# A block's seven products on TensorE reordered, so that two which share a PSUM bank never follow each other; one low part ahead of the last output sum

## The chip, the cores and the metric

The kernel runs on one core of one Trainium2 chip. The metric is the device time of one execution in microseconds; the median of three runs of the kernel before is 1206.51 us (1204.94 to 1207.25).

## The reference, cut to what matters

Two layers of a latent-token backbone, 512 tokens of width 1024. Each layer is a mixer with a gated residual and then a SwiGLU channel mixer (inner width 2816, which is 22 tiles of 128). The change is in the SwiGLU of the second layer:

```
def swiglu(h, w1, w3, w2):
    return (jax.nn.silu(h @ w1) * (h @ w3)) @ w2
...
        x = x + g2 * swiglu(modulate(rms_norm(x, norm2_g[i]), sh2, sc2), ffn_w1[i], ffn_w3[i], ffn_w2[i])
```

## The kernel before, in words

All matrices are fp32. A product is made from three TensorE matmuls per 128 rows of contraction: each operand is split into a high part (a rounded copy, made by ScalarE: "hi") and a low part (source minus high part, made by VectorE: "lo"), and hi·hi, hi·lo and lo·hi are summed in PSUM.

The function `ffn_blocks` does the second layer's SwiGLU. Of the 22 tiles of the inner width the first 3 are computed directly; for the other 19 (called blocks) `w1` and `w3` are taken together. A block is a 2 by 2 scheme of Strassen's kind: the two row blocks are `w3` and `w1`, the contraction of 1024 is cut in halves, and the 512 tokens are cut in halves (left and right, 256 each). It needs seven products instead of eight, each of 4 × 3 = 12 matmuls of 128×256. One call of `block_window` emits one block's window. `prod` emits the 12 matmuls of one product (line 1193 in every case, so a trace tells products apart by their tiles).

A window takes three PSUM tiles of one bank each (128×512 fp32): `b1` holds c11 in its left half; `b2` holds m6 in its left half and m7 in its right half; `b3` holds m5. In the order before the products are

1. c11 = a11 · left half of h (bank b1), copied out by ScalarE (line 1213)
2. m6 = s2 · T2 (bank b2), taken off q by VectorE (line 1217)
3. m5 = s1 · T1 (bank b3)
4. m7 = s3 · T3 (bank b2, right half), added into c by VectorE (line 1222); m5 is added into c as well (line 1223)
5. m6 = a22 · T4 (bank b2, left half again, a new sum), added into c by VectorE (line 1226)
6. c11 += a12 · left half of h (bank b1), through Silu on ScalarE (line 1229)
7. m5 += s4 · right half of h (bank b3); its reader (line 1234) is emitted in the next window

The text calls the fifth product "m6 again", the sixth "c11 again" and the seventh "m5 again". They are the second uses of their PSUM halves.

In the same window the weights of the next block are prepared by the list `prep` (seven steps, by index): 0 the high part of a11 and a12 (line 1133); 1 and 2 the sum s24 on VectorE (lines 1137 and 1140); 3 the low part of a11 and a12 (line 1144); 4 hi and lo of s2 and s4 (lines 96 and 97, whi and wlo of 128×1024); 5 hi and lo of s1 and s3 (lines 96 and 97); 6 hi and lo of a22 (lines 96 and 97, tile u, 128×512, in the buffers named wraw). Step 0 of the block after next is called as `after()`. `tail` holds the last three steps of the block before (lines 1234 to 1244: second Silu, product with c, hi and lo of the result).

The blocks stand in three segments of 5, 7 and 7 windows (SEGS). After each segment follow eight products with `w2` (`down`, lines 116 to 118, 24 matmuls of 128×512 or 21). In the last window of a segment, which has no next block in the segment, `prep` loads and splits the first two `w2` units instead (lines 1176 and 1180), and its step 6 is empty.

The work of this stretch is not reordered by the scheduler: `tc.manual_schedule()` is entered ahead of it, and each engine runs its instructions in the order in which the code emits them. The framework puts the semaphore waits; it tracks PSUM by tile, that is by bank, not by the half that is read.

Of the kernel before, what the change touches and what calls it, by code (L numbers as in the profile page):

```python
# [12 lines left out]
AF = mybir.ActivationFunctionType  # L13
# [8 lines left out]
HS = 256  # L22
# [39 lines left out]
def tile_dit(  # L62
# [5 lines left out]
    V, A, G, T = nc.vector, nc.scalar, nc.gpsimd, nc.tensor  # L68
# [14 lines left out]
    def ps(shape=(P, S)):  # L83
        return pp.tile([P, S], F32, tag="ps", name=nm("ps"))

    def t2k(n=S):
        return tmp.tile([P, n], F32, tag="t", bufs=TB, name=nm("t"))
# [4 lines left out]
    def f32(ap):  # L92
        return ap.bitcast(F32)
# [202 lines left out]
    for k in range(KT):  # L296
        q = acc0 if k == 0 else t2k()
# [748 lines left out]
    def ffn_blocks(l, nrm, head, sq_next=None, make_next=None):  # L1046
# [4 lines left out]
        left, right = (0, HS), (HS, S)  # L1051
# [10 lines left out]
        def gslot(f):  # L1062
            i = next(f - a for a, n in SEGS if a <= f < a + n)
            if GSL[l][i // 2] == 6:
                gt[f] = slot(("6a", "6b")[i % 2], [P, 2, S], F32R)
            elif i % 2 == 0:
                d = slot(GSL[l][i // 2], [P, 2, 2, S], F32R)
                gt[f], gt[f + 1] = d[:, 0], d[:, 1]
            return gt[f]
# [52 lines left out]
        def prep_block(f):  # L1122

            w = wf[f] = {}
            raw, s13 = raws[f], sums[f]
            a22, a11, a12 = (raw[:, q, :] for q in range(3))

            def pair(u, x, y):
                w[x], w[y] = view(u, 0), view(u, S)

            def a():
                w["ua"] = ua = hilo()
                A.copy(ua[0], raw[:, 1:3, :].rearrange("p q c -> p (q c)"))

            def b():
                w["s24"] = units.tile([P, D], F32, tag="wraw", bufs=RB, name=nm("s24"))
                V.tensor_add(w["s24"][:, :S], s13[:, :S], a11)

            def c():
                V.tensor_add(w["s24"][:, S:], a12, w["s24"][:, :S])  # L1140

            def d():
                ua = w.pop("ua")
                V.tensor_sub(ua[1], raw[:, 1:3, :].rearrange("p q c -> p (q c)"), f32(ua[0]))
                pair(ua, "a11", "a12")

            def e():
                u = hilo()
                split(*u, w.pop("s24"))
                pair(u, "s2", "s4")  # L1150

            def g():
                u = hilo()
                split(*u, s13)
                pair(u, "s1", "s3")

            def h():
                u = units.tile([P, 2, S], F32R, tag="wraw", bufs=RB, name=nm("u22"))
                split(u[:, 0, :], u[:, 1, :], a22)
                w["a22"] = view((u[:, 0, :], u[:, 1, :]), 0)  # L1160

            return [a, b, c, d, e, g, h]
# [25 lines left out]
        def prod(o, wv, bv, start=True):  # L1188
            for kk in range(4):
                wh, wl = wv(kk)  # L1190
                bh, bl = bv(kk)
                for i, (w, b) in enumerate(((wh, bh), (wh, bl), (wl, bh))):
                    T.matmul(o, w, b, start=start and kk == 0 and i == 0, stop=kk == 3 and i == 2, skip_group_check=True)  # L1193
# [4 lines left out]
        def block_window(f, tail, prep, after):  # L1198

            w = wf.pop(f)  # L1200
            hh, hl = nrm.h

            def h_op(x, half):
                return lambda kk: (hh(4 * x + kk, *half), hl(4 * x + kk, *half))

            b1, b2, b3 = ps(), ps(), ps()
            c11, m6, m7, m5 = b1[:, :HS], b2[:, :HS], b2[:, HS:], b3[:, :HS]
            q, c = t2k(), t2k()
            tail[0]()
            prep[1]()  # L1210
            tail[1]()
            prod(c11, w["a11"], h_op(0, left))
            A.copy(q[:, HS:], c11)
            prep[2]()
            tail[2]()
            prod(m6, w["s2"], st["T2"])
            V.tensor_sub(q[:, :HS], q[:, HS:], m6)
            prep[3]()
            prep[4]()
            prod(m5, w["s1"], st["T1"])  # L1220
            prod(m7, w["s3"], st["T3"])
            V.tensor_add(c[:, HS:], q[:, :HS], m7)  # L1222
            V.tensor_add(c[:, :HS], c[:, HS:], m5)
            prep[5]()
            prod(m6, w["a22"], st["T4"])
            V.tensor_add(c[:, HS:], c[:, HS:], m6)
            prep[6]()
            prod(c11, w["a12"], h_op(1, left), False)
            A.activation(q[:, HS:], c11, AF.Silu)
            after()  # L1230
            prod(m5, w["s4"], h_op(1, right), False)

            def t0():
                V.tensor_add(q[:, :HS], q[:, :HS], m5)
                A.activation(q[:, :HS], q[:, :HS], AF.Silu)

            def t1():
                V.tensor_mul(c, c, q)

            def t2():  # L1240
                d = gslot(f)
                for o, i in ((HS, 0), (0, HS)):
                    A.activation(d[:, 0, o:o + HS], c[:, i:i + HS], AF.Identity, scale=-1.0)
                    V.scalar_tensor_tensor(d[:, 1, o:o + HS], c[:, i:i + HS], -1.0, f32(d[:, 0, o:o + HS]), ALU.mult, ALU.subtract)

            return [t0, t1, t2]
# [19 lines left out]
        for a, n in SEGS:  # L1266
# [8 lines left out]
            for f in range(first, a + n):  # L1275
                i = blk.index(f)
                load_sums(i + 3)
                load_raw(i + 2)
                if f == a + n - 1:
                    prep = wprep  # L1280
                else:
                    prep = nxt_prep or prep_block(f + 1)
                    if nxt_prep is None:
                        prep[0]()
                nxt_prep = None
                after = nothing
                if f + 2 < a + n:
                    nxt_prep = prep_block(f + 2)
                    after = nxt_prep[0]
                elif f + 2 == a + n:  # L1290
                    wload, wprep = two_units(wu, [w2src(0), w2src(1)], n * P)
                    after = wload
                tail = block_window(f, tail, prep, after)
# [262 lines left out]
```

## Time and profile before

| | before |
|---|---|
| median of 3 runs | 1206.51 us |
| the profiled execution's own time | 1206.65 us |
| its span (first to last instruction) | 1204.7 us |
| TensorE busy | 1177.0 us (98%) |
| VectorE busy | 802.3 us (67%) |
| ScalarE busy | 478.3 us (40%) |
| second uses of m6 that waited for line 1222 | 19 of 19 |

Busy time of TensorE is the sum over matmuls whose rows overlap (a matmul of 128×256 has a row of 0.28 us, and the next one starts 0.12 us after it), so it says little on how densely they stand. What can be read with more trust is the time from the start of one matmul to the start of another.

### The profile page before, as it was taken

What the parts mean: (1) busy time and instruction counts of PE and PEld (TensorE: products, weight loads), DVE (VectorE), ACT (ScalarE), POOL (GpSimd) and SP (SyncE); (2) the same over time, 40 slices, a digit from 0 to 9 for tenths busy, and PEclk for the clock granted to TensorE, in tenths of its full rate; (3) what the DMA queues carried; (4) which work ended last, traced back from release to release, by engine and by line L of the source; (5) the groups of instructions that cost most, each with busy time, mean ns of one, the idle gap of its engine ahead of it and who ended that gap; (6) DMA issues with size and microseconds to landing.
All of it is one profiled execution on the core that took longest, in us unless ns stands there. A gap on an engine that the chain in (4) does not pass through costs nothing.

```text
span 1204.7 us, 16804 instructions
## 1 busy us (share of the span) xinstructions
PE 1177.0 (98%) x6627; PEld 992.8 (82%) x6627; DVE 802.3 (67%) x1302; ACT 478.3 (40%) x787; POOL 128.0 (11%) x110
## 2 busy tenths in 40 slices
PE   8999999999999999999999999999999999999998
PEld 6787856569988888888888888889998899889987
DVE  7989877657665556554443799967876467647752
ACT  5545455435332323332222554335644234324430
POOL 1013300000000000000004485100000000000000
PEclk9999999999999999999999999999999999999999
DMA  9872033383365565555455232221377156725332
GB/s 350 300 293 78 1 117 98 111 269 124 90 213 188 192 209 190 182 181 166 166 166 156 72 105 90 84 88 53 108 181 211 44 151 160 203 72 141 88 104 90
DMA packets 52226, 177.24 MB, mean 147 GB/s; under 512 B 5682, under 2 KB 6578, under 8 KB 51891
## 3 DMA queue, kind: packets, MB, share of 16 engines
q1 hardware_dynamic: 49410, 166.21, 41.7%
q0 software_dynamic: 2736, 9.96, 4.9%
q8 instruction: 52, 0.85, 0.3%
q14 instruction: 28, 0.22, 0.1%
HBM read 174.05 MB, written 2.10 MB: 146 GB/s over the span
## 4 chain that ended last, share of the span: by engine, by line
PE 92%; DVE 4%; DMA 2%; ACT 1%; issue 1%; POOL 0%; SPq 0%; DVEq 0%; ACTq 0%
PE ps L116 21%; PE ps L118 21%; PE ps L117 21%; PE ps L1193 16%; PE ps L866 2%; PE ps L708 1%; PE ps L581 1%; PE ps L851 1%; PE ps L852 1%; PE ps L853 1%; PE ps L871 1%; DMA s<-in_w 1%; DVE t L211 1%; PE ps L822 1%; PE ps L197 1%; DVE t L1222 1%
## 5 line engine op out<-in xcount | busy, mean ns | idle before, releaser
L116 PE MATMUL ps<-s,whi 128*128 128x512 f32 (+1 forms) x1067 | 394.6, 370 | 1.2 <-DVE x L272 1.2
L117 PE MATMUL ps<-s,whi 128*128 128x512 f32 (+1 forms) x1067 | 390.9, 366 | 2.1 <-DVE s L217 2.1
L118 PE MATMUL ps<-s,wlo 128*128 128x512 f32 (+1 forms) x1067 | 390.6, 366 | 0.4 <-DVE wlo L97 0.4
L96 ACT CAST whi<-wraw 128x1024 fp32r<-128x1024 f32 (+2 forms) x127 | 129.5, 1024 | 281.8 <-PE ps L117 138.1
L116 PEld LDWEIGHTS ps<-s,whi 128*128 128x128 f32 x1067 | 201.6, 189 | 35.7 <-DVE x L272 1.6
L117 PEld LDWEIGHTS ps<-s,whi 128*128 128x128 f32 x1067 | 201.7, 189 | 35.4 <-DVE s L217 2.3
L118 PEld LDWEIGHTS ps<-s,wlo 128*128 128x128 f32 x1067 | 201.6, 189 | 34.6 <-DVE wlo L97 0.9
L97 DVE TENSOR_TENSOR wlo<-wraw,whi 128x1024 fp32r<-128x1024 f32 (+2 forms) x107 | 127.1, 1188 | 80.1 <-ACT whi L96 76.6
L1193 PE MATMUL ps<-s,whi 128*128 128x256 f32 x912 | 165.2, 283 | 0.0
L1193 PEld LDWEIGHTS ps<-s,whi 128*128 128x128 f32 x912 | 142.4, 192 | 0.3
L1193 PE MATMUL ps<-s,wlo 128*128 128x256 f32 x456 | 129.0, 283 | 0.0
L272 DVE SCALAR_TENSOR_TENSOR x<-ps,m_g,x 128x512 f32<-128x512 f32 (+1 forms) x67 | 43.9, 661 | 105.7 <-PE ps L118 105.7
L154 DVE CUSTOM_DVE_ANT_0 ada<-ada,scb,vec 128x1024 f32<-128x1024 f32 x80 | 100.1, 1279 | 1.4 <-DMA ada<-in_ada 1.4
L1193 PEld LDWEIGHTS ps<-s,wlo 128*128 128x128 f32 x456 | 87.5, 192 | 0.0
L1120 POOL DMA_DIRECT2D s<-in_w x19 | 16.8, 885 | 598.6 <-DMA s<-in_w 436.5
L1008 DVE TENSOR_TENSOR t<-ps,t 128x512 f32<-128x512 f32 x22 | 15.2, 692 | 71.3 <-PE ps L118 71.3
L96 ACT CAST whi<-s 128x1024 fp32r<-128x1024 f32 x38 | 39.6, 1044 | 54.0 <-PE ps L1193 28.1
L1369 DVE SCALAR_TENSOR_TENSOR ps<-s,vec,ps 128x512 f32<-128x512 f32 x78 | 55.8, 749 | 1.4 <-ACT ps L1366 0.9
L97 POOL TENSOR_TENSOR wlo<-wraw,whi 128x1024 fp32r<-128x1024 f32 x20 | 49.0, 2454 | 31.2 <-ACT whi L96 27.2
L117 PE MATMUL ps<-s,s 128*128 128x256 f32 (+1 forms) x160 | 50.2, 315 | 0.0
L118 PE MATMUL ps<-s,s 128*128 128x256 f32 (+1 forms) x160 | 50.1, 314 | 0.0
L116 PE MATMUL ps<-s,s 128*128 128x256 f32 (+1 forms) x160 | 48.3, 317 | 0.2 <-ACT s L216 0.2
(278 smaller groups left out, 1661.0 us busy)
## 6 DMA issues: line engine op xcount, KB each, us to landing
ada<-in_ada SPq DMA_DIRECT2D x82, 512.0 KB, 4.4
wraw<-in_w SPq DMA_DIRECT2D x74, 512.0 KB, 3.6
s<-in_w SPq DMA_DIRECT2D x19, 768.0 KB, 5.7
wraw<-in_w_in SPq DMA_DIRECT2D x20, 512.0 KB, 3.3
s<-in_w SPq DMA_DIRECT2D x38, 256.0 KB, 4.0
s<-in_w POOLq DMA_DIRECT2D x19, 512.0 KB, 5.4
s<-in_ada SPq DMA_DIRECT2D x16, 512.0 KB, 6.7
wraw<-in_w_out SPq DMA_DIRECT2D x16, 512.0 KB, 3.8
```

The source lines that it names most:

```text
L96: A.copy(hi, src)
L97: (eng or V).tensor_sub(lo, src, f32(hi))
L116: T.matmul(o, wh, ah, start=start, stop=False)
L117: T.matmul(o, wh, al, start=False, stop=False)
L118: T.matmul(o, wl, ah, start=False, stop=stop)
L154: i = V.tensor_tensor_reduce(raw, raw, scv, 1.0, vc("ada_b", idx), ALU.mult, ALU.add, accum_out=dst)
L272: V.scalar_tensor_tensor(X[m][:, a:b], psum, gcol, X[m][:, a:b], ALU.mult, ALU.add)
L866: T.matmul(p[64 * x:64 * x + 64, :], vh[t][:, 2 * j + x, :], ost["p", 2 * j + x, tp][:, s * S:(s + 1) * S], start=(t == 0), stop=(t == 5))
L1008: V.tensor_mul(g, p, held.pop(f))
L1120: G.dma_start(s13, w[:, :D], accum_op=ALU.add)
L1193: T.matmul(o, w, b, start=start and kk == 0 and i == 0, stop=kk == 3 and i == 2, skip_group_check=True)
L1369: V.scalar_tensor_tensor(dst, cp[:, w:w + S], vec[:, o + w:o + w + 1], src, ALU.mult, ALU.add)
```

## The change

It moves the sixth product, c11 again, with its Silu, ahead of the fifth, m6 again. `prep[6]()` (hi and lo of a22 for the next block) now stands ahead of m6 again instead of behind it, so on VectorE the low part of a22 comes ahead of the sum that reads m6.

```diff
             V.tensor_add(c[:, HS:], q[:, :HS], m7)
             V.tensor_add(c[:, :HS], c[:, HS:], m5)
             prep[5]()
+            prod(c11, w["a12"], h_op(1, left), False)
+            A.activation(q[:, HS:], c11, AF.Silu)
+            prep[6]()
             prod(m6, w["a22"], st["T4"])
             V.tensor_add(c[:, HS:], c[:, HS:], m6)
-            prep[6]()
-            prod(c11, w["a12"], h_op(1, left), False)
-            A.activation(q[:, HS:], c11, AF.Silu)
             after()
             prod(m5, w["s4"], h_op(1, right), False)
```

Since lines move, the Silu of c11 is line 1226 in the changed kernel and line 1229 before, and the sum that reads m6 is line 1229 in the changed kernel and line 1226 before.

On TensorE, in the third window of the first segment (ps_7546 is bank b1 with c11, ps_7547 is b2 with m6 and m7, ps_7548 is b3 with m5; the tile u is a22), this stood before between the last matmul of m7 and the first of m5 again:

```order
L1193 MATMUL ps_7547<-s_1187_7213,wlo_7493 128x256
L1193 MATMUL ps_7547<-s_1188_7214,u_1237_7509 128x256 [waits DVE_49,Activation_49]
L1193 MATMUL ps_7547<-s_1190_7216,u_1237_7509 128x256
...
L1193 MATMUL ps_7546<-s_1135_6765,whi_7398 128x256 [waits Activation_49]
L1193 MATMUL ps_7546<-s_1137_6767,whi_7398 128x256
...
L1193 MATMUL ps_7548<-s_1135_6765,whi_7462 128x256 [waits DVE_49]
```

And this stands there now, at the same place of the same window:

```order
L1193 MATMUL ps_7547<-s_1187_7213,wlo_7493 128x256
L1193 MATMUL ps_7546<-s_1135_6765,whi_7398 128x256 [waits Activation_49]
L1193 MATMUL ps_7546<-s_1137_6767,whi_7398 128x256
...
L1193 MATMUL ps_7547<-s_1188_7214,u_1237_7509 128x256 [waits DVE_49]
L1193 MATMUL ps_7547<-s_1190_7216,u_1237_7509 128x256
...
L1193 MATMUL ps_7548<-s_1135_6765,whi_7462 128x256 [waits DVE_49]
```

The twelve matmuls into b1 now stand between the last matmul of m7 and the first of m6 again, which is the one that waits for VectorE; no matmul is added or removed.

On VectorE, behind the sum of m5 in the same window (t_7550 is c, u_1253 the next block's a22), the difference is:

```order
 L1223 TENSOR_TENSOR t_7550<-t_7550,ps_7548 128x256
 L97 TENSOR_TENSOR wlo_7620<-s_1207_7291,whi_7619 128x1024
-L1226 TENSOR_TENSOR t_7550<-t_7550,ps_7547 128x256
 L97 TENSOR_TENSOR u_1253_7636<-s_1225_7417,u_1253_7636 128x512
+L1229 TENSOR_TENSOR t_7550<-t_7550,ps_7547 128x256
 L1234 TENSOR_TENSOR t_7549<-t_7549,ps_7548 128x256
 L1137 TENSOR_TENSOR s_1263_7680<-s_1224_7413,s_1241_7544 128x512
```

The sum that reads m6 moved behind the low part of a22. On ScalarE, at the same place of the window (ps_7546 is c11, t_7549 is q), the difference is:

```order
 L96 CAST whi_7589<-s_1247_7553 128x1024
 L96 CAST whi_7619<-s_1207_7291 128x1024
+L1226 ACTIVATE t_7549<-ps_7546 128x256
 L96 CAST u_1253_7636<-s_1225_7417 128x512
-L1229 ACTIVATE t_7549<-ps_7546 128x256
 L1133 CAST whi_7652<-s_1241_7544 128x1024
 L1235 ACTIVATE t_7549<-t_7549 128x256
```

The Silu of c11 moved ahead of the high part of a22.

## Rows read from the trace of the kernel before

**Rows 1.** Page: shares of the chain that ended last, by engine.

```profile
PE 92%; DVE 4%; DMA 2%; ACT 1%; issue 1%; POOL 0%; SPq 0%; DVEq 0%; ACTq 0%
```

**Rows 2.** Waits of TensorE: waiter, releaser, us in total, times, longest us.

```profile
PE ps L1193 <- DVE t L1222: 11.8, 19, 0.9
```

**Rows 3.** Chain that ended last, first segment: start us, us, what.

```profile
898.33 0.43 DVE t L1222
898.89 10.31 PE ps L1193 x84
```

**Rows 4.** Timeline of TensorE, one window: start us, us, instruction, count, [idle before].

```profile
898.01 0.28 PE L1193 MATMUL ps<-s,wlo 128*128 128x256 f32 x1
898.89 1.66 PE L1193 MATMUL ps<-s,u 128*128 128x256 f32 x12 [0.60 <-DVE t L1222]
900.39 0.40 PE L1193 MATMUL ps<-s,whi 128*128 128x256 f32 x2
...
908.91 0.28 PE L1193 MATMUL ps<-s,wlo 128*128 128x256 f32 x1
```

**Rows 5.** Timeline of the weight loads at the same place.

```profile
897.89 0.19 PEld L1193 LDWEIGHTS ps<-s,wlo 128*128 128x128 f32 x1
898.86 0.30 PEld L1193 LDWEIGHTS ps<-s,u 128*128 128x128 f32 x2 [0.78 <-issue]
```

**Rows 6.** Three stretches of seven products: stretch, us, busy (count), PEclk, DMA, GB/s.

```profile
870.13:925.07 54.94, 51.62 (x420) 50.61 (x419) 1.00 0.75 197
969.54:1045.87 76.33, 72.10 (x588) 70.84 (x587) 1.00 0.68 174
1084.74:1161.07 76.33, 72.10 (x588) 70.84 (x587) 1.00 0.45 114
```

**Rows 7.** Timeline of all engines, first window of the first segment.

```profile
875.87 0.28 PE L1193 MATMUL ps<-s,wlo 128*128 128x256 f32 x1
...
876.59 0.42 DVE L1222 TENSOR_TENSOR t<-t,ps 128x256 f32<-128x256 f32 x1
...
877.06 1.10 PE L1193 MATMUL ps<-s,u 128*128 128x256 f32 x7 [0.91 <-DVE t L1222]
```

**Rows 8.** Timeline of VectorE in the window of rows 4.

```profile
895.45 0.42 DVE L1217 TENSOR_TENSOR t<-t,ps 128x256 f32<-128x256 f32 x1
...
898.33 0.42 DVE L1222 TENSOR_TENSOR t<-t,ps 128x256 f32<-128x256 f32 x1 [0.18 <-PE ps L1193]
898.78 0.42 DVE L1223 TENSOR_TENSOR t<-t,ps 128x256 f32<-128x256 f32 x1
899.34 1.23 DVE L97 TENSOR_TENSOR wlo<-s,whi 128x1024 fp32r<-128x1024 f32 x1
900.59 0.42 DVE L1226 TENSOR_TENSOR t<-t,ps 128x256 f32<-128x256 f32 x1
900.93 0.69 DVE L97 TENSOR_TENSOR u<-s,u 128x512 fp32r<-128x512 f32 x1
903.47 0.42 DVE L1234 TENSOR_TENSOR t<-t,ps 128x256 f32<-128x256 f32 x1 [1.86 <-PE ps L1193]
```

**Rows 9.** Timeline of ScalarE in the same window.

```profile
894.01 0.37 ACT L1213 COPY t<-ps 128x256 f32<-128x256 f32 x1 [0.57 <-PE ps L1193]
...
898.26 1.05 ACT L96 CAST whi<-s 128x1024 fp32r<-128x1024 f32 x1 [2.31 <-PE ps L1193]
899.21 0.62 ACT L96 CAST u<-s 128x512 fp32r<-128x512 f32 x1
902.08 0.38 ACT L1229 ACTIVATE t<-ps 128x256 f32<-128x256 f32 x1 [2.25 <-issue]
```

**Rows 10.** One period: us, then busy of PE, PEld, DVE, ACT, POOL, clock, DMA.

```profile
898.89:909.79 10.90, 10.30 (x84) 10.12 (x85) 8.66 (x15) 5.24 (x10) 0.86 (x1) 1.00 0.67 163
```

**Rows 11.** Timeline of VectorE behind the first segment (products with w2).

```profile
928.61 1.23 DVE L97 TENSOR_TENSOR wlo<-wraw,whi 128x1024 fp32r<-128x1024 f32 x1 [0.49 <-ACT whi L96]
...
936.38 0.75 DVE L272 SCALAR_TENSOR_TENSOR x<-ps,m_g,x 128x512 f32<-128x512 f32 x1 [3.68 <-PE ps L118]
```

## The prediction

> **What bounds the kernel now.** I read the page first. The chain that ended last is 92% TensorE and 4% VectorE [rows 1], and TensorE is busy in 98% of the span, so only time in which TensorE stands can be won. Next the list of TensorE's waits: the longest entry by far is line 1193 (the products of the blocks) waiting for line 1222 (the sum that reads m7), 11.8 us in 19 waits, one for each of the 19 windows [rows 2]. The chain shows the same thing in order of time: line 1222 takes 0.43 us of it, then 84 matmuls, which is one window, and then the next line 1222 [rows 3]. So in this stretch TensorE works without a break except for one hole per window, and that hole lies between m7 and m6 again.
>
> The timeline shows the hole itself [rows 4, 8]. The last matmul of m7 starts at 898.01 and its row ends at 898.29. VectorE begins line 1222 at 898.33, having idled 0.18 us for TensorE, and ends at 898.75. TensorE starts m6 again at 898.89. Nothing else is late: c11 again, which stands behind m6 again in TensorE's order, needs only weights made in the window before and the copy of c11, which began at 894.01 [rows 9], yet it starts at 900.39, when its turn comes.
>
> **What one hole costs.** The idle time in the list (0.60 us) runs from the modelled end of a matmul and so is not the price. The price is what start-to-start times give. From 900.39 to 908.91 are 71 steps without a hole (c11 again, m5 again, then c11, m6, m5 and m7 of the next window): 8.52 / 71 = 0.120 us a step [rows 4]. A full window of 84 steps would take 10.08 us. The period from m6 again to m6 again is 10.90 us [rows 10]. A hole thus costs 0.82 us: 0.76 of it between 898.01 and 898.89 (0.88 less one step), and 0.06 inside m6 again, whose twelve steps take 1.50 us and not 1.44, the start after a stand.
>
> The three stretches of product windows give the total: 54.94, 76.33 and 76.33 us for 420, 588 and 588 matmuls, which at 0.120 us would need 50.40, 70.56 and 70.56. The excess is 4.54 + 5.77 + 5.77 = 16.08 us [rows 6]. Eighteen holes of 0.82 make 14.76. The first window of the first segment has a longer one, because VectorE is still behind there: from 875.87 to 877.06 is 1.19, less a step 1.07, with the 0.06 it is 1.13 [rows 7]. Together 15.89 us; the other 0.19 of the excess are not holes of this kind and stay.
>
> The granted clock is 1.00 in all three stretches [rows 6], which is the 2.4 GHz level, so the clock has nothing to give back here.
>
> The Trainium skill (TensorE: Matmul & The Clock Gate, the engine queue's row of the table at its head) says that TensorE pulls weight loads ahead of matmuls that are still in flight. By that the weights of m6 again would be loaded when the wait ends and only the listed idle would be lost, 11.8 us in all. The trace does not agree for a product that waits: its weight load starts at 898.86, 0.97 us after the load before it and just ahead of its matmul [rows 5]. I take the start-to-start price, and keep 11.8 us as a rival.
>
> **The change, part by part.** Let M be the start of m7's last matmul (898.01 in the rows). All times below are estimates from the rows' durations.
>
> *c11 again moves ahead.* It writes bank b1, which VectorE does not read at that time. Its twelve steps start at M + 0.12 instead of waiting, so the cost is 0. Line 1222 still runs from M + 0.32 to M + 0.74, and TensorE could start m6 again at M + 0.88 [rows 4, 8]. Its turn now comes at M + 0.12 + 1.44 = M + 1.56. The hole is covered with 0.68 us to spare, 0.37 in the first window, where line 1222 starts 0.72 after M and not 0.32 and TensorE could start at M + 1.19 [rows 7]. m5 again, now at M + 3.00, waits for line 1223, which ends at M + 1.19. Gain: the 15.89 us above.
>
> *Silu ahead of a22's high part on ScalarE.* The cast of 128×1024 runs from M + 0.25 to M + 1.30 as before [rows 9]. Silu must now wait for c11 again, whose last matmul starts at M + 1.44 and ends at M + 1.72, so it runs from M + 1.76 to M + 2.14, and the cast of u (0.62) from there to M + 2.76. Before, the cast of u ended at M + 1.82 [rows 9]. So it comes 0.94 later.
>
> *a22's low part ahead of the sum of m6 on VectorE.* It cannot start before M + 2.79 and ends at M + 3.48. Line 1229 needs m6 again, which ends at M + 3.00 + 0.16 = M + 3.16, so it starts at M + 3.48 and ends at M + 3.90: the low part holds it up by some 0.3 us. The next VectorE instruction waits for m5 again, whose row ends at M + 4.32 + 0.28 = M + 4.60. VectorE is idle for some 0.7 us there, down from 1.86 [rows 8]. That idle is what hides both moves; cost 0. Should it be used up, lateness runs on to line 1217, which the next m7 waits for. Line 1217 ends at 895.87, and that m7 begins 11 steps before 898.01, at 896.69 [rows 4, 8]: another 0.8 us, so some 1.5 us of lateness cost nothing.
>
> *Shorter windows.* VectorE's 8.66 us of work per window [rows 10] now stand against 10.08 us (86%), ScalarE's 5.24 against the same. Neither becomes the bound. The DMA engines were busy 0.75, 0.68 and 0.45 of the three stretches [rows 6]; with the same bytes in 92% of the time that is 0.82 at most.
>
> *Behind the segments.* The products with w2 start 0.82 us earlier against their loads. After the first segment the third unit's low part ends at 929.84, and its product cannot start before about 936 (the second one is read at 936.38) [rows 11]: 6 us to spare. Cost 0.
>
> Sum: the profiled execution took 1206.65 us, and 1206.65 − 15.89 = 1190.8. It lies 0.14 above the median of the runs, so for the median I forecast **1190.7 us**.
>
> **Rivals.**
>
> *A, the forecast*: all 19 holes close. 1190.7; with the spread of the runs shown (−1.6 to +0.7) from 1189.1 to 1191.9.
>
> *B*: only the listed idle comes back, 11.8 us, because a change of product after a wait costs its filling anyway. 1206.5 − 11.8 = 1194.7. For it speaks that the list counts no more. Against it: between 900.39 and 908.91 the product changes five times at no cost in steps [rows 4].
>
> *C, no change*: the time won is given back behind each segment, where the products wait for w2. 1206.5. Against it are the 6 us of room [rows 11].
>
> *D, slower*: the first matmul of c11 again also has a wait, for ScalarE, which so far was hidden behind the hole. If its count is reached only with the 128×1024 cast in front of it (end M + 1.30) and not already with the copy at line 1213, TensorE starts at about M + 1.44 instead of M + 0.12 and a window loses 1.32 + 0.06 = 1.38 us in place of 0.82: 19 × 0.56 = 10.6 us more than now, 1217.1. It turns slower than before from a release later than M + 0.88. The rows before cannot exclude it, since the cast ended at 899.31 and c11 again started at 900.39 [rows 4, 9]. Against it: what the product needs of ScalarE is the copy of b1 and the weights' high part, and both stand ahead of that cast in ScalarE's order.
>
> **How the numbers follow.** A 0.85, B 0.08, C 0.04, D 0.03. A measurement of this kernel can tell about 0.2% (2.4 us) from no change. A and B are faster by more: 0.93; C is the same: 0.04; D is slower: 0.03. The range runs from A's lower end, 1189.1, to B with a little of the spread, 1195.1; C and D, 0.07, stay outside.
>
> **What would show it.** In the changed profile line 1193 should have left TensorE's waits, or stand there with under 1 us. The windows should be 10.08 us from m6 again to m6 again, and the three stretches about 50.5, 70.6 and 70.6 us. Line 1222 should still start 0.32 after the last start of m7, while twelve matmuls go on beside it. VectorE's idle time ahead of line 1234 should fall from 1.86 to some 0.7 us. The prediction is wrong if TensorE waits for ScalarE at c11 again (D), if a hole of 0.2 us stays at each m6 again (B), if line 1217 or 1234 begins to release TensorE, or if waits for w2 appear behind the segments (C).

## The result, and the profile after

The changed kernel takes 1191.04 us in the median of its four runs, before 1206.88 us in the runs beside it. One of the four took 6635.86 us, for a reason that no trace here shows, and is left out of the ratio; the other three took 1190.21, 1190.24 and 1191.84 us. The ratio is 0.987, with a 95% interval from 0.985 to 0.9889. In a second measurement the changed kernel took 1189.92 us (four runs, 1189.83 to 1190.12) against 1206.22, a ratio of 0.9863 (0.9846 to 0.9879). The forecast was 1190.7 us in a range from 1189.1 to 1195.1.

The page of the changed kernel, its span, TensorE's busy time and the chain that ended last:

```profile
span 1188.3 us, 16786 instructions
PE 1174.4 (99%) x6627; PEld 993.1 (84%) x6627; DVE 802.1 (67%) x1302; ACT 478.8 (40%) x787; POOL 127.6 (11%) x110
...
PE 94%; DVE 3%; DMA 2%; ACT 1%; issue 0%; POOL 0%; ACTq 0%; DVEq 0%; SPq 0%
```

The number of matmuls is the same and their busy time hardly moved; the span is 16.4 us shorter. The waits of TensorE now begin like this (waiter, releaser, us in total, times, longest us):

```profile
PE ps L288 <- ACT crow L132: 3.4, 1, 3.4
PE ps L117 <- DVE s L217: 2.1, 1, 2.1
```

The entry of line 1193 with 11.8 us and 19 times [rows 2] is gone. The three stretches of products, to be set beside [rows 6]:

```profile
869.58:920.33 50.75, 50.65 (x420) 50.40 (x419) 1.00 0.78 209
964.80:1035.37 70.57, 70.56 (x588) 70.51 (x587) 1.00 0.70 180
1074.23:1144.79 70.56, 70.56 (x588) 70.50 (x587) 1.00 0.47 121
```

The second and third hold 588 matmuls in 70.57 and 70.56 us, which is 0.120 us for each: TensorE does not stand there at all. Together the stretches fell from 207.60 to 191.88 us, by 15.72. Of the other 0.7 us of the span's 16.4, 0.55 lies ahead of the first stretch, which begins that much earlier than before, though nothing was changed ahead of it; most of the rest is the rounding of the two spans.

TensorE around the place of the former hole, third window of the first segment, to be set beside [rows 4]:

```profile
895.73 0.28 PE L1193 MATMUL ps<-s,wlo 128*128 128x256 f32 x1
895.85 0.40 PE L1193 MATMUL ps<-s,whi 128*128 128x256 f32 x2
...
897.29 1.60 PE L1193 MATMUL ps<-s,u 128*128 128x256 f32 x12
898.73 0.40 PE L1193 MATMUL ps<-s,whi 128*128 128x256 f32 x2
...
907.37 1.60 PE L1193 MATMUL ps<-s,u 128*128 128x256 f32 x12
```

The last matmul of m7 starts at 895.73, the first of c11 again 0.12 later, and m6 again at 897.29 without an idle time. Its twelve steps take 1.44 us (to 898.73) and no longer 1.50. From m6 again to m6 again are 10.08 us.

VectorE in the same window, to be set beside [rows 8]:

```profile
896.05 0.42 DVE L1222 TENSOR_TENSOR t<-t,ps 128x256 f32<-128x256 f32 x1 [0.19 <-PE ps L1193]
896.51 0.42 DVE L1223 TENSOR_TENSOR t<-t,ps 128x256 f32<-128x256 f32 x1
897.06 1.23 DVE L97 TENSOR_TENSOR wlo<-s,whi 128x1024 fp32r<-128x1024 f32 x1
898.47 0.69 DVE L97 TENSOR_TENSOR u<-s,u 128x512 fp32r<-128x512 f32 x1 [0.18 <-ACT u L96]
899.08 0.41 DVE L1229 TENSOR_TENSOR t<-t,ps 128x256 f32<-128x256 f32 x1
900.38 0.42 DVE L1234 TENSOR_TENSOR t<-t,ps 128x256 f32<-128x256 f32 x1 [0.88 <-PE ps L1193]
```

Line 1222 starts 0.32 us after m7's last start, as before, but now c11 again runs beside it. VectorE's idle time ahead of line 1234 is 0.88 us instead of 1.86.

ScalarE in the same window, to be set beside [rows 9] (the Silu of c11 is line 1226 now):

```profile
895.98 1.05 ACT L96 CAST whi<-s 128x1024 fp32r<-128x1024 f32 x1 [2.31 <-PE ps L1193]
897.54 0.38 ACT L1226 ACTIVATE t<-ps 128x256 f32<-128x256 f32 x1 [0.51 <-PE ps L1193]
897.82 0.61 ACT L96 CAST u<-s 128x512 fp32r<-128x512 f32 x1
```

Silu runs as soon as c11 again is done, and the cast of u behind it, 2.09 us after m7's last start; before, it stood 1.20 after it.

One place still waits. In the first window of the first segment m7 starts late (TensorE's timeline):

```profile
873.77 0.28 PE L1193 MATMUL ps<-s,wlo 128*128 128x256 f32 x1
874.15 0.50 PE L1193 MATMUL ps<-s,whi 128*128 128x256 f32 x2
```

From 873.77 to 874.15 are 0.38 us where 0.12 would do, and the first pair is stretched. The chain shows line 1217, the read of m6, just ahead of it, and ahead of that VectorE's wait for a load at the stretch's start. I had named line 1217 releasing TensorE as a sign of being wrong; it does so here, in one window of 19. The new order is not the reason: before, too, m7 of this window started right behind line 1217 (874.45, and line 1217 ended at 873.99 + 0.42 = 874.41). How long it stands depends on when the load comes. In the second profile of the changed kernel line 1217 starts 3.94 us after the stretch's start and not 4.10, and the first stretch is shorter:

```profile
869.24:919.82 50.58, 50.58 (x420) 50.39 (x419) 1.00 0.77 207
```

### The profile page after: what moved, and what is told of

It is laid out like the page before. It is cut to its first block, busy times and chain, and to the rows that moved or that the text cites. A ratio compares the mean times of both kernels' runs of the same rounds, so it can differ in the third digit from the quotient of the medians.

```text
span 1188.3 us, 16786 instructions
## 1 busy us (share of the span) xinstructions
PE 1174.4 (99%) x6627; PEld 993.1 (84%) x6627; DVE 802.1 (67%) x1302; ACT 478.8 (40%) x787; POOL 127.6 (11%) x110
## 4 chain that ended last, share of the span: by engine, by line
PE 94%; DVE 3%; DMA 2%; ACT 1%; issue 0%; POOL 0%; ACTq 0%; DVEq 0%; SPq 0%
PE ps L116 21%; PE ps L117 21%; PE ps L118 21%; PE ps L1193 16%; PE ps L866 2%; PE ps L708 1%; PE ps L581 1%; PE ps L851 1%; PE ps L852 1%; PE ps L853 1%; PE ps L871 1%; DVE t L211 1%; DMA s<-in_w 1%; PE ps L822 1%; PE ps L197 1%; PE ps L293 1%
```

## The experiments

My theory was that m6 again waits for VectorE to read m7 because both lie in bank b2, and that the gain is this hole, closed by the product that now lies between them.

**The order alone.** The products stand as in the changed kernel, and the split of a22 goes back behind the sum of m6:

```diff
             A.activation(q[:, HS:], c11, AF.Silu)
-            prep[6]()
             prod(m6, w["a22"], st["T4"])
             V.tensor_add(c[:, HS:], c[:, HS:], m6)
+            prep[6]()
```

> The products stand in the new order, but the low part of a22 stays behind the sum of m6, as before. Theory (the hole closes because c11 again lies between m7 and m6 again): as fast as the changed kernel, about 1191 us, and line 1193 gone from the waits of TensorE. Rival (the low part's new place carries part of the gain): slower than the changed kernel by more than 2 us.

Measured: 1190.46 us, ratio to before 0.9868 (0.9853 to 0.9883). The 19 waits for line 1222 are gone and the second segment's stretch is 70.56 us. One wait of line 1193 stays against what I expected, 0.4 us for line 1217 in the first window, the place that still waits in the changed kernel. The whole gain comes with the order.

**The low part alone.** The old order of products, with the split of a22 ahead of m6 again:

```diff
             prep[5]()
+            prep[6]()
             prod(m6, w["a22"], st["T4"])
             V.tensor_add(c[:, HS:], c[:, HS:], m6)
-            prep[6]()
             prod(c11, w["a12"], h_op(1, left), False)
```

> The products keep the old order; only the step that splits a22 stands ahead of m6 again. Theory: nothing is covered, 19 holes of 0.82 us from start to start stay, 1206 to 1207 us, and VectorE idles as long as before ahead of the sum of m5 again. Rival (the low part's new place helps or hurts by itself): a change of over 2 us either way.

Measured: 1206.41 us, ratio 0.9998 (0.9988 to 1.0007). TensorE's waits still hold the 19 of line 1222:

```profile
PE ps L1193 <- DVE t L1222: 11.8, 19, 0.9
```

VectorE's idle time ahead of line 1234 is 1.99 us in the third window, before 1.86. This half of the change is worth nothing by itself, in either direction, that the runs could tell from zero.

**A bank of its own for m7.** The kernel before, with its order, but four PSUM tiles per window:

```diff
-            b1, b2, b3 = ps(), ps(), ps()
-            c11, m6, m7, m5 = b1[:, :HS], b2[:, :HS], b2[:, HS:], b3[:, :HS]
+            b1, b2, b3, b4 = ps(), ps(), ps(), ps()
+            c11, m6, m7, m5 = b1[:, :HS], b2[:, :HS], b4[:, HS:], b3[:, :HS]
```

> The old order, but m7 has a bank of its own (four PSUM tiles per window instead of three). Theory (the hole is a wait for a read of the shared bank): m6 again has nothing left to wait for, the hole closes, about 1191 us. Rival (a product that follows m7 must stand whatever its bank, for instance for the end of the pipeline): 1206 to 1207 us, with holes of 0.8 us at m6 again.

Measured: 1190.35 us, ratio 0.9866 (0.9851 to 0.9881). Its three stretches (us, then busy of TensorE and its weight loads, clock, DMA):

```profile
870.09:920.48 50.39, 50.39 (x420) 50.34 (x419) 1.00 0.78 212
964.95:1035.51 70.56, 70.56 (x588) 70.52 (x587) 1.00 0.68 181
1074.38:1144.93 70.55, 70.55 (x588) 70.50 (x587) 1.00 0.47 124
```

Here m6 again follows m7 directly and does not wait. So it is the shared bank that makes the hole, and not the change of product. What is shown is the wait that the framework puts for a shared tile; no run here leaves that wait out while the bank stays shared. The first stretch has no excess either (50.39 us for 420 steps): m7 does not share with m6 any more, and so need not wait for line 1217 in the first window. In time the two ways of closing the hole cannot be told apart.

**Neighbours again.** From the changed kernel, c11 again goes one product further ahead, so that m6 again follows m7 once more:

```diff
+            prod(c11, w["a12"], h_op(1, left), False)
+            A.activation(q[:, HS:], c11, AF.Silu)
             prod(m7, w["s3"], st["T3"])
...
             prep[5]()
-            prod(c11, w["a12"], h_op(1, left), False)
-            A.activation(q[:, HS:], c11, AF.Silu)
             prep[6]()
```

> From the changed kernel, c11 again and its Silu move one product further ahead, so that m6 again follows m7 directly once more, while everything else of the change stays. Theory: the 19 holes are back, 1206 to 1207 us. Rival (an earlier c11 again, with an earlier Silu, is what pays, wherever it stands): about 1191 us.

Measured: 1204.55 us, ratio 0.9986 (0.9976 to 0.9995), that is 2 us less than before and a little below what I expected. The holes are back in all 19 windows, but they are shorter (timeline of TensorE, then of VectorE, where the sum that reads m7 is line 1224):

```profile
898.61 0.28 PE L1193 MATMUL ps<-s,wlo 128*128 128x256 f32 x1
899.40 1.70 PE L1193 MATMUL ps<-s,u 128*128 128x256 f32 x12 [0.51 <-DVE t L1224]
```

```profile
898.92 0.42 DVE L1224 TENSOR_TENSOR t<-t,ps 128x256 f32<-128x256 f32 x1 [1.62 <-PE ps L1193]
```

The sum ends at 899.34, and m6 again starts 0.06 later. Before, it was 0.14: 898.75 to 898.89 [rows 4, 8]. The stretch of the second segment is 75.95 us, against 76.33 before, which is 0.05 per window, or 1 us in 19. The profile shows two more sources of the 2 us. The first stretch is 54.32 us (before 54.94), 0.4 less than its five windows explain, since m7 comes twelve matmuls later in the first window and VectorE has caught up by then. And that stretch begins at 869.75 (before 870.13), though nothing was changed ahead of it.

**One semaphore.** What differs is the wait itself: before, the first matmul of m6 again waits on VectorE's semaphore and on ScalarE's; in the run above, on VectorE's alone. This run has the old order of products, and the split of a22 ahead of that of s1 and s3, so that an earlier wait of m5 already covers ScalarE's part:

```diff
+            prep[6]()
             prep[5]()
             prod(m6, w["a22"], st["T4"])
             V.tensor_add(c[:, HS:], c[:, HS:], m6)
-            prep[6]()
```

> The product order of before, with the split of a22 placed ahead of that of s1 and s3, so that the first matmul of m6 again waits on VectorE's semaphore alone and no longer on VectorE's and ScalarE's. Theory (the hole of 0.82 us holds some 0.05 us for the second semaphore, since the run with m6 again right behind m7 and one semaphore had a window of 10.85 us and not 10.90): windows of 10.85 us, 19 x 0.05, about 1 us less than before, 1205 to 1206. Rival (that run's shorter window came from another place of c11 again): windows of 10.90 us, no change.

Measured: 1206.31 us, ratio 0.9998 (0.9988 to 1.0007). The expected microsecond does not show in the time, whose interval (−1.4 to +0.8 us) is wide enough to hide it. It does show in the windows. The second segment's stretch, and the hole in TensorE's timeline:

```profile
970.51:1046.52 76.01, 72.33 (x588) 70.89 (x587) 1.00 0.66 170
```

```profile
899.12 0.28 PE L1193 MATMUL ps<-s,wlo 128*128 128x256 f32 x1
899.92 1.70 PE L1193 MATMUL ps<-s,u 128*128 128x256 f32 x12 [0.52 <-DVE t L1222]
...
910.77 1.46 PE L1193 MATMUL ps<-s,u 128*128 128x256 f32 x10 [0.51 <-DVE t L1222]
```

The window is 10.85 us (899.92 to 910.77), as in the run before this one, while c11 again stands where it did. The run also holds its own comparison. For the first block of the second and of the third segment the split of a22 is still the last one, and m6 again keeps both waits there. In the first window of the second segment

```profile
976.15 0.28 PE L1193 MATMUL ps<-s,wlo 128*128 128x256 f32 x1
977.03 1.67 PE L1193 MATMUL ps<-s,u 128*128 128x256 f32 x12 [0.60 <-DVE t L1222]
```

are 0.88 us from start to start, as before, and not 0.80. So 16 windows changed and not 19, since the very first one has a single wait in the kernel before, too. In the first segment, however, the profiled execution is longer than before (55.97 us against 54.94), which takes the gain back. There VectorE waits for a load at the start and reaches line 1217 5.08 us after the stretch's start (875.15 and 870.07), not 3.86 as in the kernel before (873.99 and 870.13). That wait lies ahead of the first instruction that was moved.

**A longer VectorE.** In the changed kernel and in the one before, the low part of s2 and s4 is made twice, the same values:

```diff
             def e():
                 u = hilo()
-                split(*u, w.pop("s24"))
+                s24 = w.pop("s24")
+                split(*u, s24)
+                V.tensor_sub(u[1], s24, f32(u[0]))
```

> The changed kernel once more, in five rounds, to narrow the interval and as the reference for the runs beside it: 1190 to 1192 us.

> The changed kernel, in which VectorE makes the low part of s2 and s4 twice (one more operation on 128x1024, about 1.15 us, ahead of line 1222, in 16 of 19 windows). Theory (c11 again covers the first 0.68 us of lateness, and VectorE is ahead of TensorE by 0.18): a hole of 1.15 - 0.18 - 0.68, about 0.3 us, plus 0.06 for the start, in 16 windows: 5 to 6 us slower than the changed kernel, about 1196 to 1197. Rival (VectorE, at 97% of a window of 10.08 us, becomes the bound): 12 us slower or more. Second rival (VectorE has no influence any more): no change.

> The same doubled operation in the kernel before, where nothing covers line 1222. Theory: each of 16 holes grows by 1.15 - 0.18, about 0.97 us, so 15 to 16 us slower than the kernel before, about 1222. Rival (the hole is of fixed length, set by TensorE): no change, 1206 to 1207.

Measured: the changed kernel 1189.92; with the longer VectorE 1194.59, that is 4.7 us more, a little under the 5 to 6 expected. The kernel before 1206.22; with the longer VectorE 1223.23, that is 17.0 more, over the 15 to 16 expected. In the profiles part of both differences lies ahead of the first stretch, where only one of the extra operations stands: the stretch begins at 868.60 us instead of 869.24 in the changed kernel, and at 871.23 instead of 870.13 in the kernel before. The three stretches together grew by 5.37 us (191.70 to 197.07) and by 15.66 (207.60 to 223.26). So the same operation costs about three times as much where nothing covers line 1222. In the changed kernel with it (timeline of VectorE, then of TensorE; line 1224 reads m7):

```profile
895.53 1.23 DVE L1151 TENSOR_TENSOR wlo<-s,whi 128x1024 fp32r<-128x1024 f32 x1
896.67 0.42 DVE L1224 TENSOR_TENSOR t<-t,ps 128x256 f32<-128x256 f32 x1
```

```profile
896.80 0.28 PE L1195 MATMUL ps<-s,wlo 128*128 128x256 f32 x1
897.14 1.70 PE L1195 MATMUL ps<-s,u 128*128 128x256 f32 x12
898.68 0.40 PE L1195 MATMUL ps<-s,whi 128*128 128x256 f32 x2
```

Line 1224 ends at 897.09, past the end of c11 again, and m6 again starts 0.34 us after the last start instead of 0.12 and then takes 1.54 us instead of 1.44. That makes 0.32 in this window; over the second segment it is 72.54 − 70.57 = 1.97 us for six windows with the operation, 0.33 each, for 0.36 expected. In the kernel before with the longer VectorE (all engines):

```profile
901.89 0.61 ACT L96 CAST u<-s 128x512 fp32r<-128x512 f32 x1
902.00 0.41 DVE L1224 TENSOR_TENSOR t<-t,ps 128x256 f32<-128x256 f32 x1
...
902.56 1.67 PE L1195 MATMUL ps<-s,u 128*128 128x256 f32 x12 [1.59 <-ACT u L96]
```

The trace names ScalarE's cast as the releaser, because it ended last. But that cast makes the next block's a22. TensorE starts 0.15 us after line 1224's end at 902.41, nearly the same distance as before (0.14). In the kernel before, m6 again started at 898.89 while that cast ended only at 899.83 [rows 4, 9], so it does not need the cast: VectorE released it. Each of the six windows with the operation in the second segment grew by (82.37 − 76.33) / 6 = 1.01 us, for 0.97 expected.

## Why the prediction was right

**The hole and its cause.** Shown from both sides: where m6 again follows m7 in one bank, the hole is there in every order tried, and a bank of its own or a product between them removes it. Rival D, a wait of c11 again for ScalarE's cast, did not come: c11 again starts at 895.85, and that cast ends at 895.98 + 1.05 = 897.03.

**Its price.** By start-to-start times I had 15.89 us for the holes; the stretches fell by 15.72. The difference of 0.17 is in the first window, where 0.35 us of excess stayed (50.75 for 50.40) and I had left 0.19. It is m7's wait for line 1217, and it changes with the load: in the second profile of the same kernel the excess is 0.18 (50.58), and the stretches, 191.70 us in all, are 15.90 below those of before. That close an agreement is in part luck, since it hangs on when one load comes. Rival B, the listed idle of 11.8 us, is refuted: had only that come back, the stretches would still hold 4 us of excess. The Trainium skill's rule (TensorE: Matmul & The Clock Gate, the engine queue's row in its opening table) that weight loads are pulled ahead did not apply to a product that waits: in the run with neighbours again, too, the first weight load and the first matmul of m6 again are both listed at 899.40. In the changed kernel, where m6 again does not stand, the trace agrees with it: its first weight load starts at 897.18, its first matmul at 897.29.

**What hides the moves.** The estimates from M (here 895.73) held to 0.13 us: Silu, u's low part and line 1229 were put at M + 1.76, 2.79 and 3.48 and line 1234 not ahead of M + 4.60, and they stand at M + 1.81, 2.74, 3.35 and 4.65. VectorE's idle ahead of line 1234 came out at 0.88 us for 0.7: u's low part came 0.05 us earlier than put, line 1229 started 0.08 ahead of the end of that row (899.08, and 898.47 + 0.69 = 899.16), and line 1234 came 0.05 later. The spare time of 0.68 us under c11 again was tested with an operation longer than that, and the remainder appeared as a hole of the expected size.

**Behind the segments.** Nothing was given back (rival C): the times between the stretches are 44.47 and 38.86 us, before 44.47 and 38.87.

What is not settled: 0.55 us of the profiled span lie ahead of the first stretch, where no instruction changed; the repeated runs of the kernel before differ by more than that, and over the ten profiles the first stretch begins anywhere from 868.60 to 871.23.

## What to carry to other kernels

When a product waits for a sum that only reads the other half of its bank, look for a product already in the window whose operands are ready and whose bank nobody reads, and put it between; if banks are free, a bank of its own does the same and leaves the order alone. Price such a wait by start-to-start times of the matmuls, not by the idle time that the list of waits gives, which here showed 11.8 of 15.7 us. Then count the slack of the engine that does the reading: covered by 1.44 us of products, the same extra VectorE operation cost 0.33 us per window instead of 1.01, but not nothing.

## What the runs showed that I had not expected

The hand-over to TensorE was longer where the waiting matmul waits on two semaphores: 0.14 us from the end of the sum to the first start with VectorE's and ScalarE's, 0.06 and 0.05 us with VectorE's alone, although ScalarE's had been reached long before. The kernel before has a case of each: in its very first window m6 again waits on VectorE's alone, and there it is 0.05 us (876.59 + 0.42 = 877.01, and 877.06 [rows 7]). Per window it was 0.05 us (10.90 and 10.85), since the twelve steps behind it were then 0.03 longer (1.53 us, before 1.50). Two runs with different orders of products agree on it; their medians do not resolve it as a time of the kernel. The trace also shows what the second semaphore adds: waits that stand as instructions of their own on line 1193, of 51 ns each. There are 22 in the kernel before, and 6 in the run with one semaphore, which is 16 fewer, one for each window that became shorter (before, then that run; instruction, count, shortest, median and longest ns, first and last start us):

```profile
L1193 PEldq EVENT_SEMAPHORE  x22: 51/51/51, 866.1 to 1156.6; - x22
L1193 PEldq EVENT_SEMAPHORE  x6: 51/51/51, 866.0 to 1091.8; - x6
```

That these 51 ns are the price is argued from their number and size; no run adds such an instruction alone.
